# Gated-delta heads with beta as rows, two wide decay sums and block-wise inverse joins, and a relative-bias table written in eight pieces beside the weight loads

## The chip, the cores and the metric

The kernel runs on one core of a Trainium2 chip. The metric is the device time of one execution in microseconds (us), the median of several runs; lower is better. The core has five engines with a program each: TensorE (PE) multiplies matrices, VectorE (DVE), ScalarE (ACT) and GpSimd (POOL) work elementwise, and SyncE (SP) issues most of the transfers. Sixteen DMA engines carry the transfers between DRAM and the on-chip memory (SBUF); products land in PSUM.

## The reference, cut to what matters

An input x of 512 positions by 2048 features goes through three blocks in float32: (1) a gated recurrence and dilated attention, (2) spatial gating and neighbourhood attention, (3) a gated delta rule with 8 heads and sliding-window attention with 16 heads and a relative bias. Blocks 2 and 3 are modulated by `silu(c) @ w_ada + b_ada`. The change concerns parts of block 3:

```python
def gated_delta_rule_chunked(q, k, v, g, beta):
    g = jnp.cumsum(chunk(g), axis=-1)
    gdiff = g[..., :, None] - g[..., None, :]
    decay = jnp.where(causal, jnp.exp(jnp.where(causal, gdiff, 0.0)), 0.0)
    k_beta = k * beta[..., None]
    L = jnp.where(strict, einsum("bnhid,bnhjd->bnhij", k_beta, k) * decay, 0.0)
    t_inv = triangular_solve(eye + L, eye, lower=True, unit_diagonal=True)
    k_dec = k * jnp.exp(g_last[..., None] - g)[..., None]
    ...
def sliding_window_attention(q, k, v, sinks, rel_bias):
    bias = rel_bias[t5_bucket(jnp.maximum(dist, 0))]     # 32 buckets x 16 heads
    logits = where(valid, logits + bias, -inf)
    ...
```

## The kernel before, in words

All activations stand transposed, as 16 tiles of 128 features by 512 positions. Nearly all of PE's time goes into projections. `unit_steps` makes one tile of 128 outputs from 16 input tiles: two calls of `wchunk` each load 8 blocks of 128x128 weights (512 KB, `wr`, three buffers) on SP's queue; ACT rounds each half of 512 columns to `wh` (L114), DVE takes the rest as `wl` (L117; five halves of each fit), and PE multiplies three times per input tile (L128): `wh` by the high and the low part of the input, `wl` by the high one. A unit is 48 products of 128x512, a chunk 24.

`drive` runs a list of Python generators, one per head or gate. A generator yields either a unit that it needs or nothing; `drive` emits a unit's products, lets the waiting generators take a step between groups of 12 products, and so writes a head's small operations between the products of other units. The order of SP's queue, in which a transfer that waits holds up all behind it, comes out of the same program and the tile framework, which adds the waits for data and for buffers.

Beside this, each `wchunk` calls `bg()`, which takes one step of the first generator in `bgq`: before the change, `mods` for block 2 and then for block 3. Each of their steps loads 512 KB of `w_ada` (`gr`, two buffers) and adds it to `ga` (one buffer) on DVE.

`rel_bias` (L1279 on) is called at the start of `block2` (L798). It loads a one-hot table, the 32x16 bias and a mask, makes a 16x384 table of the biases by head and distance with one product and one sum, and writes each of the 16 rows 128 times to DRAM (`reld`, 16x128x384, 3 MB) with one DMA on ACT's queue. Much later `swa` (L1303 on) reads from `reld` with rows 383 apart, so that each of 128 positions finds its biases shifted by one.

In block 3, positions are in 4 chunks of 128 (`n`), and a tile of 128x512 holds the four chunks of a head side by side. `gdn_scalars` works out beta, g and the exponentials of its sums for all heads as columns (128 positions by 4 chunks x 8 heads). `gdn_k` (L1030 on) runs once per head: the keys are convolved, turned (`tr4`, four transposes, L134) and normalised to `kn`; POOL multiplies them by beta (`kb`) and by the decay to the chunk's end (`kd`); DVE multiplies a triangular matrix by g, chunk by chunk (`gt`); after two steps PE turns `kn` and `kb` and multiplies `later` (a constant triangle) by `gt` in four float32 products, whose exponential is the decay `dec`; then `at` is the strict triangle L. `inverse_blocks` solves the 32x32 diagonal blocks for two heads at a time on DVE, by way of DRAM (`du`, then `fs`; the result through `tm` to `dt`, and into `e0`). `inverse_join` joins these blocks to the inverse of 128x128: `c1` and `c2` are L with all but the blocks of one level set to zero, made on POOL by two mask products (L1128, L1129); each level is a chain of products of 128x128x128 in float32, four at a time, and sums on DVE. `gdn_scan` then goes through the four chunks of the head one after the other.

The functions that the change touches, and what calls them, with the line numbers of the profile:

Of the kernel before, what the change touches and what calls it, by code (L numbers as in the profile page):

```python
# [10 lines left out]
F32 = mybir.dt.float32  # L11
F32R = mybir.dt.float32r
# [3 lines left out]
OP = mybir.AluOpType  # L16
AX = mybir.AxisListType.X

P = 128
T = 512  # L20
# [20 lines left out]
class Kernel:  # L41
    def __init__(self, ctx, tc, A, outs, stop=99):
        self.tc, self.nc, self.A, self.O, self.stop = tc, tc.nc, A, outs, stop
        nc = self.nc
# [14 lines left out]
        C = self.A["const"]  # L59
# [17 lines left out]
        self.gld = self.dp.tile([2 * KT, P, T], F32, name="gld")  # L77
        self.reld = self.dp.tile([16, P, 384], F32, name="reld")
        self.res = self.dp.tile([KT, P, T], F32, name="res")


    def col(self, name, k=0, n=1):
# [475 lines left out]
                self.bg()  # L558

    def drain_bg(self):  # L560
        while self.bgq:
            self.bg()

    def mods(self, wada, c, b, mod):

# [229 lines left out]
    def block2(self, h, first):  # L795
        w = self.A["w2"]
        ys = [None] * 16
        self.rel_bias()  # L798
        todo = [self.sgu(g, h, w, ys) for g in range(8)]
        for p in range(8):  # L800
            todo.append(self.na(p, h, w, ys))
            if p:
                todo.append(self.gate(ys, 7 + p, w, 47 + p, h))
        todo.append(self.gate(ys, 15, w, 55, h))
        self.drive(todo, WIDTH2, done=first)
        return ys
# [157 lines left out]
    def gdn_scalars(self, ba):  # L964

        nc = self.nc
# [14 lines left out]
        self.log1p_cols(e, e)  # L981
        self.stt(gx, gx, 0.0, e, OP.max, OP.add)
        self.stt(c8(gx), c8(gx), -1.0, ea[:, None, :].to_broadcast([P, 4, 8]))
        ps = self.x()
        self.mm(ps[:, 0:32], self.triu, gx)
        self.mm(ps[:, 32:64], self.ones, gx)
        self.mm(ps[:, 64:96], self.later, gx)
        self.g, self.egc, self.egl, self.edl = gx, C("egc"), C("egl"), C("edl")
# [5 lines left out]
        self.ts(self.bh, beta, 0.5)  # L994

    def conv(self, ps, i):

# [31 lines left out]
    def gdn_k(self, hd, h, w, ks, free):  # L1029
        nc = self.nc  # L1030
        while not free():
            yield
        k = self.conv((yield w, 8 + hd, h), 8 + hd)
        yield
        yield
        kt = self.tr4(k)
        ss, rk = self.s(4), self.s(4)
        sq = self.t()
        self.act(sq, kt, AF.Square)
        nc.vector.tensor_reduce(ss, sq.rearrange("p (n t) -> p n t", t=P), AX, OP.add)  # L1040
# [24 lines left out]
        nc.gpsimd.affine_select(dec.rearrange("p (n t) -> p n t", t=P), dec.rearrange("p (n t) -> p n t", t=P),  # L1065
                                [[0, 4], [1, P]], OP.is_ge, 0.0, base=0, channel_multiplier=-1)
        yield
        gm = self.x()
        for n in range(4):
            c = slice(n * P, (n + 1) * P)  # L1070
            self.mm(gm[:, c], kf[:, c], kbf[:, c])
        at = self.y()
        self.tt(at, gm, dec)
        ks[hd] = kf, kd, dec, at

    def inverse_blocks(self, ats, e0s):
# [3 lines left out]
        nc = self.nc  # L1080
        self.n += 1
        B = 16 * len(ats)
        fs = self.gp.tile([P, 1024], F32, name=f"fs{self.n}", tag="gr", bufs=2)
        pr = self.gp.tile([P, 256], F32, name=f"fp{self.n}", tag="fp", bufs=1)
        tm = self.gp.tile([P, 256], F32, name=f"ft{self.n}", tag="ft", bufs=1)
        du = self.dp.tile([B, 1024], F32, name=f"du{self.n}")
# [30 lines left out]
                    e0s[a][32 * b:32 * b + 32, :].rearrange("c (n i) -> c n i", i=P)[:, :, 32 * b:32 * b + 32],  # L1117
                    dt[p0:p0 + 4].rearrange("n (c i) -> c n i", i=32))

    def inverse_join(self, at, e0):  # L1120

        nc = self.nc
        m = lambda i: self.mask_c[:, None, i * P:(i + 1) * P].to_broadcast([P, 4, P])
        v4 = lambda a: a.rearrange("p (n t) -> p n t", t=P)
        e, f = e0, self.t()
        nc.vector.transpose(f, e0)
        c1, c2 = self.t(), self.t()
        nc.gpsimd.tensor_tensor(v4(c1), v4(at), m(0), OP.mult)  # L1128
        nc.gpsimd.tensor_tensor(v4(c2), v4(at), m(1), OP.mult)  # L1129
        for lv, c in ((0, c1), (1, c2)):  # L1130
            yp, zp = self.x(), self.x()
            sl = [slice(n * P, (n + 1) * P) for n in range(4)]
            for q in sl:
                self.mm(yp[:, q], c[:, q], f[:, q])
            y = self.t()
            self.act(y, yp)
            yield
            for q in sl:
                self.mm(zp[:, q], y[:, q], e[:, q])
            if lv == 0:  # L1140
                zt = self.x()
                for q in sl:
                    self.mm(zt[:, q], e[:, q], y[:, q])
                f1, e1 = self.t(), self.t()
                self.tt(f1, f, zt, OP.subtract)
                self.tt(e1, e, zp, OP.subtract)
                f, e = f1, e1
                yield
            else:
                self.tt(e, e, zp, OP.subtract)  # L1150
        return e

    def gdn_qv(self, hd, h, w, ks, qs):
# [70 lines left out]
    def gdn(self, h, w, ys):  # L1224
# [18 lines left out]
        def scan(a):  # L1243
# [1 line left out]
                yield  # L1245
            kf, kd, dec, at = ks[a]
            q, rq, vb = qs[a]
            e = yield from self.inverse_join(at, f0s[a])
            yield
            ys[a] = yield from self.gdn_scan(a, kf, kd, e, q, rq, dec, vb)  # L1250

# [26 lines left out]

    def rel_bias(self):  # L1279
        nc = self.nc  # L1280
        ld, rb = self.t(), self.s(16)
        nc.sync.dma_start(ld[0:32, 0:384], self.A["rel1h"])
        nc.sync.dma_start(rb[0:32], self.A["rel"])
        mk = self.t()
        nc.sync.dma_start(mk[0:16, 0:384], self.A["relmask"])
        ps = self.x()
        self.mm(ps[0:16, 0:384], rb[0:32], ld[0:32, 0:384])
        self.tt(mk[0:16, 0:384], ps[0:16, 0:384], mk[0:16, 0:384], OP.add)
# [289 lines left out]
```

## Time and profile before

| | |
|---|---|
| runs, median (lowest to highest) | 3489.82 us (3487.78 to 3497.07), 3 runs |
| the profiled execution, its own time | 3486.6 us |
| its span in the profile | 3484.9 us |
| mean clock that PE was granted | 0.989 |
| moved by DMA | 449.39 MB |

The profile's first page gives each engine's busy time and share of the span, and the chain of work that ended last, as shares of the span by engine and line. Further views of the trace group instructions by line and tile, list the chain or the instructions in order of time, and give the busy times of a stretch. In them, a name such as `wl<-wr,wh` is the output and the inputs of an instruction by the program's tile names, L117 is a line of the kernel, `x4` is a count, and a float32 product appears as two records of PE. `PEld` is the load of weights into PE. In the rows of DMA issues the last number is the median time from issue to landing.

### The profile page before, as it was taken

The page shows a single profiled execution, that of the slowest core. Times are in us where ns is not written, and L with a number is a line of the kernel's source. Part 1 is how long each engine was busy: PE and PEld are TensorE (multiplying, and loading weights), DVE is VectorE, ACT ScalarE, POOL GpSimd, SP SyncE. Part 2 cuts the span into 40 slices and gives each one's busy share as a digit, 9 for nine tenths or more (in the row PEclk, how much of TensorE's full clock was granted, in tenths as well). Part 3 has the DMA queues.
Part 4 walks back from the last instruction along what each step waited for, and adds up shares of the span by engine and source line. Part 5 has one row for each costly group of instructions (what it writes and reads, how often), then busy time and mean ns, then how long its engine had stood idle before and what let it go on. Part 6 is the DMA issues. An engine that isn't in the chain of part 4 may idle for free.

```text
span 3484.9 us, 44515 instructions
## 1 busy us (share of the span) xinstructions
PE 3400.8 (98%) x16678; PEld 2841.0 (82%) x16678; DVE 2008.9 (58%) x3496; ACT 1273.6 (37%) x2439; POOL 322.9 (9%) x278
## 2 busy tenths in 40 slices
PE   8999999999999899999999999999999999999999
PEld 6878888888887788888888788787878888888887
DVE  8677656556767456644368767656754433344552
ACT  4222244444434222544442243232334443432331
POOL 3000000000341000101103201111110000000000
PEclk9999999999999999999999999999999999999999
DMA  6354355435564645522234233222222233324442
GB/s 219 115 169 158 129 167 177 142 131 184 199 218 134 154 161 187 172 87 91 87 102 145 91 120 91 88 90 79 81 70 79 91 102 101 128 97 145 144 142 91
DMA packets 157640, 449.39 MB, mean 129 GB/s; under 512 B 25792, under 2 KB 35824, under 8 KB 157424
## 3 DMA queue, kind: packets, MB, share of 16 engines
q1 hardware_dynamic: 155216, 442.96, 38.5%
q10 hardware_dynamic: 2208, 3.59, 0.8%
q8 instruction: 131, 2.15, 0.3%
q14 instruction: 85, 0.70, 0.1%
HBM read 421.31 MB, written 25.17 MB: 128 GB/s over the span
## 4 chain that ended last, share of the span: by engine, by line
PE 87%; DVE 6%; issue 3%; DMA 3%; POOL 1%; ACT 1%; SPq 0%; DVEq 0%; ACTq 0%; POOLq 0%
PE pm L128 75%; PE x L128 8%; DMA gr<-in_wada_dram 2%; PE x L134 2%; PE x L527 1%; DVE wl L117 1%; DVE t L117 1%; DVE ga L120 1%; DVE fp L117 1%; DMA wr<-in_w_dram 1%; DVE t L120 1%; DVE ft L1109 0%; POOL s L142 0%; DMA t<-in_xt_dram 0%; ACT t L114 0%
## 5 line engine op out<-in xcount | busy, mean ns | idle before, releaser
L128 PE MATMUL pm<-a,wh 128*128 128x512 f32 x8512 | 2673.4, 395 | 15.2 <-ACT a L114 15.2
L128 PEld LDWEIGHTS pm<-a,wh 128*128 128x128 f32 x8512 | 1578.4, 189 | 333.3 <-ACT a L114 17.2
L128 PE MATMUL pm<-a,wl 128*128 128x512 f32 x4256 | 1668.6, 392 | 8.7 <-DVE wl L117 8.7
L117 DVE TENSOR_TENSOR wl<-wr,wh 128x512 fp32r<-128x512 f32 (+1 forms) x1080 | 764.9, 711 | 1005.3 <-ACT wh L114 940.4
L114 ACT ACTIVATE wh<-wr 128x512 fp32r<-128x512 f32 (+1 forms) x1080 | 675.9, 628 | 1767.0 <-PE pm L128 1622.6
L128 PEld LDWEIGHTS pm<-a,wl 128*128 128x128 f32 x4256 | 803.0, 189 | 182.7 <-DVE wl L117 10.5
L120 DVE SCALAR_TENSOR_TENSOR ga<-gr,sc_c,ga 128x1024 f32<-128x1024 f32 x180 | 237.8, 1321 | 78.6 <-DMA gr<-in_wada_dram 78.2
L128 PEld LDWEIGHTS x<-t,t 128*128 128x128 f32 (+2 forms) x1488 | 187.9, 188 | 31.9 <-issue 9.4
L128 PE MATMUL x<-t,t 128*128 128x64 f32 (+3 forms) x1488 | 200.6, 277 | 5.2 <-DVE t L117 4.9
L114 ACT ACTIVATE t<-x 128x512 f32<-128x512 f32 (+3 forms) x325 | 155.8, 496 | 117.5 <-PE x L128 61.3
L142 POOL TENSOR_TENSOR s<-s,nhalf 128x4 f32<-128x4 f32 (+1 forms) x51 | 60.1, 1178 | 1289.8 <-DVE s L125 1258.3
L114 ACT ACTIVATE t<-t 128x512 f32<-128x512 f32 (+1 forms) x172 | 106.8, 630 | 134.2 <-DVE t L120 83.2
L117 DVE TENSOR_TENSOR t<-t,t 128x512 f32<-128x512 f32 (+1 forms) x195 | 137.8, 707 | 23.0 <-ACT t L114 19.0
L114 ACT ACTIVATE t<-t,s 128x128 f32<-128x128 f32 (+2 forms) x192 | 98.6, 514 | 79.4 <-DVE s L438 60.2
L134 PE MATMUL x<-cst,t 128*128 128x128 f32 x496 | 74.3, 276 | 24.0 <-ACT t L114 9.8
L134 PEld LDWEIGHTS x<-cst,t 128*128 128x128 f32 x496 | 60.6, 142 | 40.0 <-ACT t L114 10.2
L597 POOL TENSOR_TENSOR acc<-acc,t 128x512 f32<-128x512 f32 x42 | 75.7, 1828 | 85.4 <-DVE t L120 71.3
L117 DVE TENSOR_TENSOR a<-t,a 128x512 fp32r<-128x512 f32 x112 | 79.3, 727 | 4.6 <-ACT a L114 4.4
L527 PE MATMUL x<-cst,t 128*128 128x128 f32 x464 | 74.5, 275 | 4.6 <-ACT t L114 4.6
L748 POOL TENSOR_TENSOR t<-cst,t 128x256 f32<-128x256 f32 x48 | 41.2, 891 | 351.7 <-DMA t<-in_rpb_dram 274.2
L114 ACT ACTIVATE t<-pm 128x512 f32<-128x512 f32 (+2 forms) x154 | 68.6, 482 | 13.5 <-PE pm L128 13.3
L120 DVE SCALAR_TENSOR_TENSOR t<-t,pm 128x512 f32<-128x512 f32 x64 | 43.7, 684 | 46.4 <-PE pm L128 46.0
(216 smaller groups left out, 1815.6 us busy)
## 6 DMA issues: line engine op xcount, KB each, us to landing
wr<-in_w_dram SPq DMA_DIRECT2D x380, 512.0 KB, 3.3
gr<-in_wada_dram SPq DMA_DIRECT2D x192, 512.0 KB, 4.2
wr<-in_wo_dram SPq DMA_DIRECT2D x96, 512.0 KB, 3.4
wr<-in_w_dram SPq DMA_DIRECT2D x48, 256.0 KB, 2.9
t<-in_xt_dram SPq DMA_DIRECT2D x32, 256.0 KB, 4.0
res<-t SPq DMA_DIRECT2D x32, 256.0 KB, 2.2
t<-res SPq DMA_DIRECT2D x32, 256.0 KB, 2.8
gld<-t SPq DMA_DIRECT2D x32, 256.0 KB, 2.0
```

Source lines behind the costliest of these rows:

```text
L114: return self.nc.scalar.activation(out, in_, fn, **kw)
L117: return self.nc.vector.tensor_tensor(out, a, b, op)
L120: return self.nc.vector.scalar_tensor_tensor(out, a, s, b, op0=op0, op1=op1)
L128: return self.nc.tensor.matmul(out, l, r, start=start, stop=stop, skip_group_check=True)
L134: self.nc.tensor.transpose(b[:, p * P:(p + 1) * P], src[:, p * P:(p + 1) * P], self.ident)
L142: self.nc.gpsimd.tensor_tensor(out, u, self.nhalf[:, :n], OP.pow)
L527: self.nc.tensor.transpose(b[:, j * P:(j + 1) * P], pr[:, j * P:(j + 1) * P], self.ident)
L597: self.nc.gpsimd.tensor_tensor(self.acc[i], self.acc[i], src, OP.add)
L748: nc.gpsimd.tensor_tensor(rows(nbs[hh][cb]), self.mask_na[:, None, v * 32:v * 32 + 32].to_broadcast([P, 8, 32]), sv[:, :, off:off + 32], O ...
```

## The change

The diff, cut to its core:

```diff
     def drain_bg(self):
-        while self.bgq:
-            self.bg()
+        for q in self.bgq:
+            for _ in q:
+                pass
+        self.bgq = []
...
     def block2(self, h, first):
-        self.rel_bias()
...
     def gdn_scalars(self, ba):
+        pads = self.gp.tile([P, 1024], F32, name="pads", tag="gr", bufs=2)
+        nc.gpsimd.memset(pads, 0.0)
+        self.pads = [pads[:, 0:T], pads[:, T:]]
+        gr = self.gp.tile([P, 1024], F32R, name="later_r", tag="gr", bufs=2)
+        self.later_r, self.ghl = gr[:, 0:P], [gr[:, P:P + 32], gr[:, P + 32:P + 64]]
+        nc.vector.tensor_copy(self.later_r, self.later)
+        nc.vector.tensor_copy(self.ghl[0], gx)
+        self.tt(self.ghl[1], gx, self.ghl[0].bitcast(F32), OP.subtract)
...
+        nc.tensor.transpose(pt[0:32, 0:P], beta, self.ident)
+        nc.vector.tensor_copy(rt[0:32, 0:P], pt[0:32, 0:P])
+        nc.sync.dma_start(self.betad.rearrange("n h t -> (n h) t"), rt[0:32, 0:P])
+
+    def beta_row(self, hd):
+        r = self.t()
+        src = self.betad
+        self.nc.sync.dma_start(r.rearrange("p (n t) -> p n t", t=P),
+                               bass.AP(tensor=src.tensor, offset=src.offset + hd * P,
+                                       ap=[[0, P], [8 * P, 4], [1, P]]))
+        return r
...
     def gdn_k(self, hd, h, w, ks, free):
+        br = self.beta_row(hd)
...
-        kb = self.t()
-        nc.gpsimd.tensor_tensor(kb.rearrange("p (n d) -> p n d", d=P), kn.rearrange("p (n d) -> p n d", d=P),
-                                self.hc(self.beta, hd)[:, :, None].to_broadcast([P, 4, P]), OP.mult)
-        kd = self.y()
-        nc.gpsimd.tensor_tensor(kd.rearrange("p (n d) -> p n d", d=P), kn.rearrange("p (n d) -> p n d", d=P),
-                                self.hc(self.edl, hd)[:, :, None].to_broadcast([P, 4, P]), OP.mult)
-        gt = self.t()
-        for n in range(4):
-            self.ts(gt[:, n * P:(n + 1) * P], self.triu, self.g[:, 8 * n + hd:8 * n + hd + 1])
+        gts = [self.t("w", F32R) for _ in range(2)]
+        for gt, g in zip(gts, self.ghl):
+            self.tt(gt.rearrange("p (n t) -> p n t", t=P), self.triu[:, None, :].to_broadcast([P, 4, P]),
+                    self.hc(g, hd).bitcast(F32)[:, :, None].to_broadcast([P, 4, P]))
         yield
         yield
         kf, kbf = self.y(), self.t()
         self.act(kf, self.tr4(kn))
-        self.act(kbf, self.tr4(kb))
...
-        for n in range(4):
-            c = slice(n * P, (n + 1) * P)
-            self.mm(gb[:, c], self.later, gt[:, c])
+        for i in range(2):
+            self.mm(gb, self.later_r, gts[i], start=i == 0, stop=i == 1)
...
+        self.tt(kbf, kf, br)
+        kd = self.y()
+        self.rows(kd, kn, self.hc(self.edl, hd))
...
     def inverse_blocks(self, ats, e0s):
-        fs = self.gp.tile([P, 1024], F32, name=f"fs{self.n}", tag="gr", bufs=2)
+        fs = self.gp.tile([P, 1024], F32, name=f"fs{self.n}", tag="ga", bufs=1)
...
-    def inverse_join(self, at, e0):
-        nc.gpsimd.tensor_tensor(v4(c1), v4(at), m(0), OP.mult)
-        nc.gpsimd.tensor_tensor(v4(c2), v4(at), m(1), OP.mult)
-        for lv, c in ((0, c1), (1, c2)):
...
+    def inverse_join(self, at, e, c):
+        f = self.t()
+        nc.vector.transpose(f, e)
+        for r in (0, 64):
+            self.act(v4(c)[r:r + 32, :, r + 32:r + 64], v4(at)[r:r + 32, :, r + 32:r + 64])
+        yp, zp, zt = self.x(), self.x(), self.x()
+        for q in sl:
+            self.mm(yp[:, q], c[:, q], f[:, q])
+        self.act(y, yp)
+        yield
+        for n, q in enumerate(sl):
+            self.mm(zt[:, n * P:n * P + 64], e[:, q], y[:, n * P:n * P + 64])
+        for q in sl:
+            self.mm(zp[:, q], y[:, q], e[:, q])
+        self.ts(v4(f)[32:64, :, 0:32], v4(zt)[32:64, :, 0:32], -1.0)
+        for r in (0, 64):
+            self.ts(v4(e)[r:r + 32, :, r + 32:r + 64], v4(zp)[r:r + 32, :, r + 32:r + 64], -1.0)
+        yield
+        for n in range(4):
+            self.mm(b[64:128, 64 * n:64 * n + 64], at[0:64, n * P + 64:n * P + P], f[0:64, n * P:n * P + 64])
+        self.act(y2[64:128, 0:256], b[64:128, 0:256])
+        yield
+        for n in range(4):
+            self.mm(b[0:64, 64 * n:64 * n + 64], y2[64:128, 64 * n:64 * n + 64], e[64:128, n * P + 64:n * P + P])
+        self.ts(v4(e)[0:64, :, 64:128], b[0:64, 0:256].rearrange("p (n t) -> p n t", t=64), -1.0)
...
     def rel_bias(self):
+        buf = self.gp.tile([P, 1024], F32, name="relb", tag="ga", bufs=1)
+        mk, ld, rb = buf[0:16, 0:384], buf[0:32, 384:768], buf[0:32, 768:784]
...
+        yield
+        yield
...
-        nc.scalar.dma_start(self.reld, mk[0:16, None, 0:384].to_broadcast([16, P, 384]))
+        for i in range(0, 16, 2):
+            yield
+            nc.sync.dma_start(self.reld[i:i + 2], buf[i:i + 2, None, 0:384].to_broadcast([2, P, 384]))
...
     def run(self):
+        self.bgq.append(self.rel_bias())
         h, first = self.out1(self.block1())
         h, first = self.out2(self.block2(h, first))
+        self.drain_bg()
```

In words. Beta goes to DRAM once (`betad`, 16 KB), and each head reads its row into all 128 partitions, so that it can be multiplied into the turned keys; four transposes and a copy per head fall away, and both products with beta and with the end decay move from POOL to DVE. g is split into a high and a low fp32r part, and the four float32 products of the decay sum become two fp32r products of 512 columns. The first level of the join takes its blocks by two ACT copies into tiles that were set to zero once; the second level multiplies 64x64 blocks only, and results are written, negated, just where they belong. The buffer `fs` of the solves moves to the tag `ga`, of which there is one. `rel_bias` becomes the third background generator: it starts when both `mods` are done, in block 2's attention part, and issues its eight pieces of two rows each (384 KB) on SP's queue, one per background step.

What SP issues there now, in the order of its program (`wr_...` are weight loads, with the program's number; the three `relb` loads are the table's inputs, and `t<-in_rpb_dram` belongs to the neighbourhood attention). First up to the load 12756:

```order
L157 DMA wr_12664<-in_w_dram 128x1024
L157 DMA wr_12701<-in_w_dram 128x1024
L1307 DMA relb<-in_rel1h_dram 32x384
L1308 DMA relb<-in_rel_dram 32x16
L1309 DMA relb<-in_relmask_dram 16x384
L746 DMA t_12744<-in_rpb_dram 128x384
L157 DMA wr_12756<-in_w_dram 128x1024
L746 DMA t_12750<-in_rpb_dram 128x384
```

And right behind these rows:

```order
L157 DMA wr_12838<-in_w_dram 128x1024
L157 DMA wr_12924<-in_w_dram 128x1024
L1318 DMA reld<-relb 256x1x384 x4
L157 DMA wr_12974<-in_w_dram 128x1024
L1318 DMA reld<-relb 256x1x384
L157 DMA wr_13035<-in_w_dram 128x1024
L1318 DMA reld<-relb 256x1x384
L157 DMA wr_13070<-in_w_dram 128x1024
L1318 DMA reld<-relb 256x1x384
L157 DMA wr_13118<-in_w_dram 128x1024
L1318 DMA reld<-relb 256x1x384
L157 DMA wr_13153<-in_w_dram 128x1024
```

Before, the same place of SP's queue holds weight loads alone (`wr_12757` there is `wr_12756` above), and the one write stands in ACT's queue at the start of block 2, between two of its copies. First SP, then ACT:

```order
L156 DMA wr_12757<-in_w_dram 128x1024
L156 DMA wr_12838<-in_w_dram 128x1024
L156 DMA wr_12923<-in_w_dram 128x1024
L156 DMA wr_12972<-in_w_dram 128x1024
L156 DMA wr_13032<-in_w_dram 128x1024
L156 DMA wr_13066<-in_w_dram 128x1024
```
```order
L114 ACTIVATE t_9301<-pm_8825 128x512
L114 ACTIVATE t_9376<-pm_8826 128x512
L1290 DMA reld<-t_9259 2048x1x384
L114 ACTIVATE t_9417<-pm_9327 128x512
L114 ACTIVATE wh_512_9430<-wr_9424 128x512
```

Four pieces stand together behind the load 12924, and each of the four loads after it, 12974 to 13118, has one more piece behind it; the load 13153 has all eight ahead of it. PE multiplies the bias table between the weights of two chunks; `wh_0_12666` below is the first half of the load 12664:

```order
L129 MATMUL pm_12578<-a_9194,wh_512_12623 128x512
L129 MATMUL pm_12578<-a_9193,wl_512_12624 128x512
L129 MATMUL x_12674<-relb 16x384
L129 MATMUL pm_12663<-a_8833,wh_0_12666 128x512
L129 MATMUL pm_12663<-a_8834,wh_0_12666 128x512
```

So the sum that the first piece waits for can be made when PE begins the chunk of 12664, and the loads 12664, 12701, 12756, 12838 and 12924 stand ahead of the pieces in SP's queue.

The second place is PE at the key step of the first head. Before (`t_17378` is `kn`, `t_17380` is `kb`, `t_17384` is `gt`):

```order
L128 MATMUL pm_17330<-a_16688,wl_512_17396 128x512
L134 MATMUL x_17425<-cst,t_17378 128x128 x4
L134 MATMUL x_17431<-cst,t_17380 128x128 x4
L128 MATMUL x_17437<-t_17384,cst 128x128 x4
L128 MATMUL pm_17453<-a_16313,wh_0_17456 128x512
```

And now:

```order
L129 MATMUL pm_17347<-a_16694,wl_512_17410 128x512
L135 MATMUL x_17439<-cst,t_17397 128x128 x4
L129 MATMUL x_17445<-t_17399,later_r 128x512
L129 MATMUL x_17445<-t_17400,later_r 128x512
L129 MATMUL pm_17462<-a_16319,wh_0_17465 128x512
```

Twelve small PE instructions between the units' products became four small and two wide ones.

More of the change, by code (lines that the diff above doesn't have):

```diff
@@ L79, in __init__ @@
         self.res = self.dp.tile([KT, P, T], F32, name="res")
+        self.betad = self.dp.tile([4, 8, P], F32, name="betad")
     def col(self, name, k=0, n=1):
@@ L987, in gdn_scalars @@
         self.mm(ps[:, 64:96], self.later, gx)
-        self.g, self.egc, self.egl, self.edl = gx, C("egc"), C("egl"), C("edl")
+        self.egc, self.egl, self.edl = C("egc"), C("egl"), C("edl")
         self.act(self.egc, ps[:, 0:32], AF.Exp)
@@ L994, in gdn_scalars @@
         self.ts(self.bh, beta, 0.5)
+        pt, rt = self.x(), self.t()
+        nc.tensor.transpose(pt[0:32, 0:P], beta, self.ident)
[8 more added lines that the diff above has]
+        return r
     def conv(self, ps, i):
@@ L1118, in inverse_blocks @@
                     dt[p0:p0 + 4].rearrange("n (c i) -> c n i", i=32))
-    def inverse_join(self, at, e0):
+    def inverse_join(self, at, e, c):
         nc = self.nc
-        m = lambda i: self.mask_c[:, None, i * P:(i + 1) * P].to_broadcast([P, 4, P])
         v4 = lambda a: a.rearrange("p (n t) -> p n t", t=P)
[L1125 to L1128, printed above, removed]
-        nc.gpsimd.tensor_tensor(v4(c2), v4(at), m(1), OP.mult)
-        for lv, c in ((0, c1), (1, c2)):
[L1131 to L1150, printed above, removed]
@@ new lines, in inverse_join @@
+        f = self.t()
[3 more added lines that the diff above has]
+        yp, zp, zt = self.x(), self.x(), self.x()
+        sl = [slice(n * P, (n + 1) * P) for n in range(4)]
+        for q in sl:
+            self.mm(yp[:, q], c[:, q], f[:, q])
+        y = self.t()
+        self.act(y, yp)
+        yield
+        for n, q in enumerate(sl):
+            self.mm(zt[:, n * P:n * P + 64], e[:, q], y[:, n * P:n * P + 64])
@@ new lines, in inverse_join @@
+        for q in sl:
[4 more added lines that the diff above has]
+        yield
+        b = self.x()
+        y2 = self.t()
+        for n in range(4):
+            self.mm(b[64:128, 64 * n:64 * n + 64], at[0:64, n * P + 64:n * P + P], f[0:64, n * P:n * P + 64])
+        self.act(y2[64:128, 0:256], b[64:128, 0:256])
@@ L1151, in inverse_join @@
+        yield
+        b = self.x()
+        for n in range(4):
+            self.mm(b[0:64, 64 * n:64 * n + 64], y2[64:128, 64 * n:64 * n + 64], e[64:128, n * P + 64:n * P + P])
+        self.ts(v4(e)[0:64, :, 64:128], b[0:64, 0:256].rearrange("p (n t) -> p n t", t=64), -1.0)
         return e
@@ L1247, in scan @@
             q, rq, vb = qs[a]
-            e = yield from self.inverse_join(at, f0s[a])
+            e = yield from self.inverse_join(at, f0s[a], self.pads[a % 2])
             yield
@@ L1280, in rel_bias @@
         nc = self.nc
[L1281 to L1285, printed above, removed]
-        ps = self.x()
-        self.mm(ps[0:16, 0:384], rb[0:32], ld[0:32, 0:384])
-        self.tt(mk[0:16, 0:384], ps[0:16, 0:384], mk[0:16, 0:384], OP.add)
-        nc.scalar.dma_start(self.reld, mk[0:16, None, 0:384].to_broadcast([16, P, 384]))
+        buf = self.gp.tile([P, 1024], F32, name="relb", tag="ga", bufs=1)
+        mk, ld, rb = buf[0:16, 0:384], buf[0:32, 384:768], buf[0:32, 768:784]
+        nc.sync.dma_start(ld, self.A["rel1h"])
+        nc.sync.dma_start(rb, self.A["rel"])
+        nc.sync.dma_start(mk, self.A["relmask"])
+        yield
+        yield
+        ps = self.x()
+        self.mm(ps[0:16, 0:384], rb, ld)
+        self.tt(mk, ps[0:16, 0:384], mk, OP.add)
+        for i in range(0, 16, 2):
+            yield
+            nc.sync.dma_start(self.reld[i:i + 2], buf[i:i + 2, None, 0:384].to_broadcast([2, P, 384]))
     def swa_k(self, i, h, w, kf, scale):
```

## The prediction

> **What bounds the kernel now.** I read the page's busy shares first, then the chain of work that ended last, then the places where the chain leaves TensorE (PE).
>
> ```profile
> PE 3400.8 (98%) x16678; PEld 2841.0 (82%) x16678; DVE 2008.9 (58%) x3496; ACT 1273.6 (37%) x2439; POOL 322.9 (9%) x278
> PE 87%; DVE 6%; issue 3%; DMA 3%; POOL 1%; ACT 1%; SPq 0%; DVEq 0%; ACTq 0%; POOLq 0%
> ```
>
> PE is the bound: 3484.9 - 3400.8 = 84 us of idle in the whole span. So an edit pays in two ways only: it shortens work in PE's queue, or it shortens one of the few waits. The profiled execution took 3486.6 us, of which 1.7 lie outside the span; the median of the runs is 3489.8, 0.1% above it. All sums are made against 3486.6.
>
> Two waits matter here. The first stands at the start of block 2, in the chain in order of time and in the busy times by stretch (columns: PE, PEld, DVE, ACT, POOL busy, granted clock, share of the DMA engines, GB/s):
>
> ```profile
> 1145.38 1.92 DVE wl L117 x4
> 1147.30 18.08 DMA wr<-in_w_dram
> ...
> 1148.00:1156.00 8.00, 8.00 (x38) 6.60 (x36) 0.47 (x1) 0.00 (x0) 0.00 (x0) 1.00 0.88 101
> 1156.00:1167.00 11.00, 1.19 (x6) 0.73 (x5) 1.99 (x3) 2.67 (x5) 0.00 (x0) 0.68 0.82 221
> 1167.00:1172.00 5.00, 5.00 (x18) 4.09 (x17) 3.43 (x14) 0.59 (x2) 1.01 (x1) 0.68 0.47 166
> ```
>
> A weight load took 16 to 18 us, because the DMA engines were 88% busy with something else at only 101 GB/s. PE lived on converted weights until 1156 and then sat idle for 11.00 - 1.19 = 9.8 us; afterwards its clock was 0.68 for 5 us, that is half speed for some 3.2 us, another 1.6 us lost. The something else is the relative-bias write on the ACT queue (q10), beside what the same load takes in a free moment:
>
> ```profile
> q10 hardware_dynamic: 1006, 1.55, 87.6%
> reld<-t ACTq DMA_DIRECT2D x1, 3072.0 KB
> wr<-in_w_dram SPq DMA_DIRECT2D x5, 512.0 KB, 9.9
> wr<-in_w_dram SPq DMA_DIRECT2D x380, 512.0 KB, 3.3
> ```
>
> The first row is the queue in the 15 us from 1130 to 1145: 1006 rows of 1536 bytes kept 87.6% of 16 engines, so one row held its engine for 0.876 * 16 * 15 / 1006 = 209 ns; the whole of it, 3072 KB at 101 GB/s, is 31 us.
>
> The second place is the gated-delta stage:
>
> ```profile
> 2100.00:2624.00 524.00, 501.52 (x2643) 423.69 (x2642) 351.21 (x730) 168.93 (x303) 74.28 (x83) 0.99 0.26 82
> PE x L134 <- DVE t L120: 6.4, 1, 6.4
> 2183.18 0.18 DVE L117 TENSOR_TENSOR fp<-ft,fs 128x16 f32<-128x16 f32 x1 [4.14 <-POOL ft L1099]
> 2183.69 1.63 POOL L1128 TENSOR_TENSOR t<-t,cst 128x512 f32<-128x512 f32 x1
> 2184.09 1.28 DVE L117 TENSOR_TENSOR fp<-ft,fs 128x24 f32<-128x24 f32 x1
> 2185.62 1.02 DVE L117 TENSOR_TENSOR fp<-ft,fs 128x32 f32<-128x32 f32 x1
> ```
>
> PE idles 22.5 of 524 us there. The longest wait, 6.4 us, is for VectorE (DVE), whose small products take 1.28 and 1.02 us while GpSimd (POOL) multiplies the masks, after 0.18 us just before.
>
> **The change, part by part.**
>
> *Relative bias taken out of the start of block 2.* The ACT-queue write goes, and the wait of 9.8 us and the slow clock of 1.6 us with it: -11.4 us. The load that was late is issued at 1146.1 and, at 3.3 us, lands six microseconds before PE runs dry. Bounds: 0, if another wait takes its place, and -13.
>
> *Decay sums and key products, per head.* In PE's timeline a head's key step reads:
>
> ```profile
> 2108.75 1.03 PE L134 MATMUL x<-cst,t 128*128 128x128 f32 x8
> 2109.62 1.06 PE L128 MATMUL x<-t,cst 128*128 128x128 f32 x8
> 2110.43 0.48 PE L128 MATMUL pm<-a,wh 128*128 128x512 f32 x1
> 1532.43 24.52 PE pm L128 x108
> ```
>
> From start to start, eight transposes take 0.87 us, and the four decay sums 0.81 (each float32 product is two records). Four transposes go: 0.43. Two wide products at 24.52 / 108 = 0.227 us take the place of 0.81: 0.36 saved. Eight heads times 0.79: -6.3 us, all in PE's queue. On DVE two wide products replace four narrow ones and two products come over from POOL; their cover is DVE's 33% of idle time in this stage. The row of betas is a 256 KB load per head on SP, issued two steps ahead of its use:
>
> ```profile
> t<-gld SPq DMA_DIRECT2D x32, 256.0 KB, 2.9
> ```
>
> Another load of that size lands in 2.9 us, and a step is twelve products of 0.227 us, so the two steps hide it and I cost it at nothing. If that cover fails it holds up DVE for a microsecond or two per head.
>
> *Inverse joins.* There are 20 products before and 20 after. What shrinks is their width, and a narrower one is not cheaper:
>
> ```profile
> 1417.99 1.00 PE L128 MATMUL x<-t,t 128*128 128x64 f32 x8
> 1418.82 0.61 PE L527 MATMUL x<-cst,t 128*128 128x128 f32 x4
> ```
>
> Eight records of 64 columns take 0.83 us, as against 0.81 to 0.87 for 128. Products with 64 rows and 64 weight columns in a burst are not in the trace: free at best, which saves 16 records * 0.104 * 8 heads = 13 us, and 0 at worst. I take -1, by the nearest row.
>
> *Waits of this stage.* The mask products leave POOL, so the 6.4 us wait loses its two stretched DVE steps, some 2 us. Against that, the loads of the second solve now wait for the first solve to end, since they share one buffer. I take -4, between +8 (a few waits like that one again) and -15.
>
> *The relative-bias rows, in eight pieces.* They move to block 2's attention part, onto SP's queue, which also carries every weight load. The order in the part on the change shows four pieces together, then one ahead of each of the next four loads. What does one piece cost? It has 256 rows of 1536 bytes, but its outer dimension is 2, where the old write had 16. The trace has one other DMA with a small outer dimension, the store of the solved blocks (L1112, outer dimension 4). The queue's row for half a microsecond in which that store was alone:
>
> ```profile
> 2178.47 0.66 SPq L1112 DMA_DIRECT2D dt<-ft  x1
> DMA packets 16, 0.02 MB, mean 33 GB/s; under 512 B 0, under 2 KB 16, under 8 KB 16
> q1 hardware_dynamic: 16, 0.02, 22.9%
> ```
>
> 22.9% of 16 engines is 3.7: four of them worked, twelve stood still, while the write with 16 kept 88% busy. So I take it that a piece runs on two engines, 128 rows on each. The time of a row lies between the crowded 209 ns above and an unhindered one, from a quiet stretch of weight loads:
>
> ```profile
> 2300.00:2320.00 20.00, 20.00 (x90) 16.57 (x89) 7.51 (x12) 6.12 (x10) 0.00 (x0) 1.00 0.28 92
> ```
>
> 0.28 of 16 engines for 92 GB/s is 49 ps per byte, so 75 ns for 1536 bytes and 199 for 4096. Sixteen readers crowded the old write and two crowd a piece, so I choose a value nearer to the free one: 110 ns. A piece is then 128 * 110 = 14.1 us, eight are 113 us one after the other if they share the same two engines, which I take, and every weight load behind them in the queue needs those two as well.
>
> [...]
>
> What hides it? PE computes the bias just ahead of load 12664's weights. From there PE has five chunks whose loads were issued before the pieces (12664 to 12924), and the four that follow (12974 to 13118) are loaded between pieces. The period of a chunk comes from the next like point of the chain:
>
> ```profile
> 1584.71 24.52 PE pm L128 x108
> ```
>
> From 1532.43 (quoted above) it is 52.28 us for four units of two chunks, 6.53 us each. Nine chunks are 58.8 us of cover. The load behind the last piece (13153) is usable after 113 + 5 loads * 8 rows * 0.2 us (8) + 1.5 (product, sum, issue) + 1.7 (landing) + 0.6 (conversion) = 124.8 us. PE is short by 66 us, in some five waits, and loses about 1.6 more to the clock at the end, as at 1167. Cost: +67 us. Bounds: 75 ns per row give 77 + 12 - 59 + 2 = +32; 209 ns give 214 + 12 - 59 + 2 = +169; all sixteen engines, at the old write's 31 us in all, give 0.
>
> **Sum.** 3486.6 - 11.4 - 6.3 - 1 - 4 + 67 = **3531 us**, slower by 1.2% of the median.
>
> **The rivals.**
>
> *The pieces hide (faster).* If a piece ran on all 16 engines, or each on a pair of its own, eight would take some 31 us, less than the cover. The point from which it decides is (58.8 - 11.8) / 8 = 5.9 us per piece: below, PE never waits. Then only the gains stay: 3486.6 - 22.7 = 3464.
>
> ```profile
> gr<-in_wada_dram SPq DMA_DIRECT2D x192, 512.0 KB, 4.2
> ```
>
> For it speaks that 192 such loads, each larger than a piece, ran through the same queue and landed in 4.2 us; against it the 22.9%.
>
> *Crowded rows.* A row costs 209 ns whoever else reads: 3486.6 - 22.7 + 169 = 3633. Against it: the old crowd was sixteen engines.
>
> *Free rows.* 75 ns: 3486.6 - 22.7 + 32 = 3496, no change that can be seen. [...]
>
> *DVE becomes the bound of the gated-delta stage.* It takes two products from POOL, and in the worst stretches it is 96% busy (19.14 of 20 us):
>
> ```profile
> 2360.00:2380.00 20.00, 18.44 (x87) 14.37 (x85) 19.14 (x45) 4.29 (x8) 0.00 (x0) 1.00 0.30 93
> ```
>  With the pieces hidden and two waits like the 6.4 us one more, 3464 + 4 + 13 = 3481.
>
> *The joins do not get shorter on PE.* That is my forecast already (-1 of a possible -13).
>
> **How the numbers follow.** The forecast, two engines at 90 to 140 ns a row, 3510 to 3562 by the same sum: 0.64. Free rows, 3485 to 3510: 0.13. Crowded rows, above 3562: 0.07. The pieces hide, 3452 to 3479: 0.12. Hidden, but DVE binds, about 3481: 0.04. The measurement can tell about 0.3%, 10 us, from no change. Faster by more than that, below 3479: 0.12. Within it, up to some 3500: the DVE case and two thirds of the free rows, 0.13. Slower: 0.75. The range runs from 3470 to 3570: the forecast, the free rows, the DVE case and the nearer edges of the other two, about 0.84. The forecast's own range is 3510 to 3562.
>
> **What would show it.** Right: after the relative-bias product, PE idle for tens of microseconds with the wait put down to `wr<-in_w_dram`, DMA engines about an eighth busy (2 of 16) in that stretch, the load behind the four pieces landing after 50 us or more; no late load at the start of block 2; two wide products of 0.45 us per head. Wrong: pieces landing within 6 us, or loads that land while pieces are still under way. The forecast fails most easily on the time of a row on two engines, then on the cover of nine chunks.

## The result, and the profile after

| | before | after |
|---|---|---|
| median of the runs, us | 3488.8 (4 runs, 3482.8 to 3497.07) | 3524.02 (4 runs, 3518.53 to 3526.41) |
| ratio to before, 95% interval | | 1.0101 [1.0087, 1.0115] |
| profiled execution, us | 3486.6 | 3518.53 |

The changed kernel is 1.0% slower. The first page of its profile gives the busy time of each engine and the shares of the chain that ended last:

```profile
PE 3394.8 (97%) x16599; PEld 2828.4 (80%) x16599; DVE 1997.4 (57%) x3508; ACT 1274.8 (36%) x2447; POOL 285.9 (8%) x247
PE 86%; DVE 6%; DMA 4%; issue 1%; SPq 1%; ACT 1%; POOL 0%; DVEq 0%; ACTq 0%; POOLq 0%
```

PE has 6 us less to do than before and is idle for 3516.8 - 3394.8 = 122 us, where it was 84. The projections are the same 12960 products in both kernels, in the same order, so the two traces can be laid beside each other: the start of a given product after, less its start before, shows where time is won or lost (worked out from the starts of the products in the traces, us):

| part of the program | change there |
|---|---|
| up to the old write (no edit acts there) | -7.8 |
| start of block 2, the old write | -13.2 |
| block 2 up to the bias product | +1.4 |
| the eight pieces | +73.9 |
| from there to the gated-delta stage | -0.2 |
| gated-delta stage | -21.8 |
| to the end | -0.1 |
| sum | +32.3 |

The first line is the scatter of single executions: in the profiles of the experiments below, that point came from 1.4 us earlier to 9.5 us later than in the profile of before, with the same instructions ahead of it. So the parts below are compared between like products, and whole kernels by the ratio of their runs.

The chain of work in order of time (start, length, what) at the place of the pieces; L1318 is their line:

```profile
1523.80 0.55 DVE relb L118
...
1524.37 0.79 SPq L1318
1525.16 0.06 issue
1525.21 4.73 SPq L1318
1529.94 0.04 issue
1529.99 15.20 SPq L1318
1545.19 0.04 issue
1545.23 15.01 SPq L1318
...
1560.35 91.12 DMA wr<-in_w_dram x5
...
1652.23 1.22 PE pm L129 x2
```

The third and the fourth piece hold SP for 15.2 and 15.0 us. By the pace of the rows below a piece takes 15.4 us, so I read the length of these issues as the time of a piece; that the queue takes no more until earlier rows are gone is my guess at the reason and was not tried by itself. The later pieces are issued in about 2 us each, but there the weight load ahead of each one holds SP, for 13 to 15 us. Then the chain is five weight loads, 91 us, until PE goes on at 1652.2. What PE does meanwhile, by its rows in order of time (in brackets the idle time before and what ended it), and then the waits and the busy times of that stretch (columns of the last row: stretch, length, PE, PEld, DVE, ACT, POOL, granted clock, share of the DMA engines, GB/s):

```profile
1589.45 1.22 PE L129 MATMUL pm<-a,wh 128*128 128x512 f32 x2 [28.97 <-ACT wh L115]
...
1593.22 0.62 PE L129 MATMUL pm<-a,wh 128*128 128x512 f32 x2
...
1605.67 1.22 PE L129 MATMUL pm<-a,wh 128*128 128x512 f32 x2 [8.86 <-ACT wh L115]
...
1621.11 1.22 PE L129 MATMUL pm<-a,wh 128*128 128x512 f32 x2 [7.69 <-ACT wh L115]
```
```profile
ACT wh L115 <- DMA wr<-in_w_dram: 65.4, 6, 27.5
...
PE pm L129 <- ACT wh L115: 60.3, 5, 29.0
```
```profile
1550.00:1660.00 110.00, 48.91 (x179) 37.86 (x179) 18.77 (x28) 15.92 (x35) 6.43 (x6) 0.67 0.24 70
```

Five waits, 60.3 of 110 us, put down to ACT's conversion, which itself waited 65.4 us for the loads. And the DMA queue of SP in 10 us (1530 to 1540) in which nothing but pieces moved: packets, MB, share of 16 engines:

```profile
q1 hardware_dynamic: 166, 0.25, 11.3%
```

11.3% of 16 is 1.8 engines; 166 rows in 10 us on two of them are 120 ns a row, and 256 rows at that pace are 15.4 us.

At the start of block 2 nothing is late any more. The old stretch in the changed kernel, and the loads in it:

```profile
1140.00:1170.00 30.00, 30.00 (x138) 24.82 (x137) 12.28 (x29) 7.81 (x14) 1.01 (x1) 0.95 0.29 94
wr<-in_w_dram SPq DMA_DIRECT2D x5, 512.0 KB, 3.2
```

The clock column of this profile reads 0.95 here, where PE is never idle; in the profile before it reads 1.00 in such a place. The products do not show a difference: 320 us of the same work (from 1180 before, from 1159 after) keep PE busy for 319.5 and 319.1 us. So I take nothing from that column when I compare these two profiles.

The key step and a join of the gated-delta stage, from the chain in order of time:

```profile
2162.93 0.45 PE x L135 x4
2163.38 0.46 PE x L129 x2
...
2245.91 1.11 PE x L129 x8
2247.03 0.93 PE pm L129 x4
2247.96 2.43 PE x L129 x24
2250.38 1.38 PE pm L129 x5
2251.76 0.60 PE x L129 x8
```

Four transposes and two wide products now take 0.91 us, where eight transposes and four float32 sums took 1.68. The second level of a join, eight records of 64x64, takes 0.60, where eight of 128x128 took 0.81 to 0.87.

### The profile page after: what moved, and what is told of

Read it like the earlier page. It is cut to its first block, busy times and chain, and to the rows that moved or that the text cites. A ratio compares the mean times of both kernels' runs of the same rounds, so it can differ in the third digit from the quotient of the medians.

```text
span 3516.8 us, 44344 instructions
## 1 busy us (share of the span) xinstructions
PE 3394.8 (97%) x16599; PEld 2828.4 (80%) x16599; DVE 1997.4 (57%) x3508; ACT 1274.8 (36%) x2447; POOL 285.9 (8%) x247
## 4 chain that ended last, share of the span: by engine, by line
PE 86%; DVE 6%; DMA 4%; issue 1%; SPq 1%; ACT 1%; POOL 0%; DVEq 0%; ACTq 0%; POOLq 0%
PE pm L129 75%; PE x L129 8%; DMA wr<-in_w_dram 3%; PE x L135 2%; DMA gr<-in_wada_dram 1%; PE x L528 1%; DVE wl L118 1%; SPq L1318 1%; DVE t L118 1%; DVE fp L118 1%; DVE t L121 1%; DVE ft L1130 1%; DVE ga L121 1%; ACT t L115 0%; ACT wh L115 0%
## 5 line engine op out<-in xcount | busy, mean ns | idle before, releaser
L129 PE MATMUL pm<-a,wh 128*128 128x512 f32 x8512 | 2677.2, 396 | 75.4 <-ACT wh L115 60.3
L129 PEld LDWEIGHTS x<-t,t 128*128 128x128 f32 (+3 forms) x1296 | 156.2, 183 | 26.6 <-issue 6.5
L129 PE MATMUL x<-t,t 128*128 128x64 f32 (+5 forms) x1296 | 167.7, 274 | 3.6 <-DVE t L118 3.6
L115 ACT ACTIVATE t<-t 128x512 f32<-128x512 f32 (+1 forms) x172 | 106.8, 630 | 120.5 <-DVE t L121 73.9
L129 PE MATMUL x<-acc,t 128*128 128x128 f32 (+3 forms) x336 | 72.8, 310 | 0.0
```

Source lines behind the costliest of these rows:

```text
L115: return self.nc.scalar.activation(out, in_, fn, **kw)
L129: return self.nc.tensor.matmul(out, l, r, start=start, stop=stop, skip_group_check=True)
```

## The experiments

Each ratio is to runs of the kernel before on the same chip. The theory at the start: the pieces cost what they do because few DMA engines serve them, with every weight load queued behind; the rest of the change gains. That the few engines set the pace did not hold, as the rows apart show.

**The relative-bias edit alone.** The kernel before, with only this:

```diff
-        self.rel_bias()                      # in block2
+        self.bgq.append(self.rel_bias())     # in run, rel_bias as in the change
```

> The kernel before with the relative-bias edit alone (third background generator, eight pieces on SP's queue); the gated-delta stage is as before. Theory: the pieces cost what the trace of the changed kernel shows between like products (73.9 us from the bias product on, less 13.2 us at the start of block 2), whatever the gated-delta stage does: 3488.8 + 61 = 3550 us, PE idle for some 60 us in several waits behind the pieces. Rival: the stall comes out of the whole change (buffers shared by the new parts): then near 3477 us.

Measured: 3553.57 us, 1.0176 [1.0151, 1.0200]. Between like products the pieces cost 72.9 us and the start of block 2 gained 13.2. The cost does not come out of the gated-delta edits.

**The gated-delta edits alone.** The changed kernel with the old `rel_bias`:

```diff
-        self.bgq.append(self.rel_bias())
+        self.rel_bias()                      # in block2, one write on ACT's queue
```

> The changed kernel with rel_bias put back as it was (one write on ACT's queue at the start of block 2); the gated-delta edits stay. Theory: the gated-delta stage keeps its 22 us of gain and the old wait at the start of block 2 comes back: 3488.8 - 22 = 3467 us. Rival: part of those 22 us is the luck of one execution (an unchanged part before block 2 was 7.8 us shorter as well): 3474 to 3478 us, which would be the forecast's own 11.3 us.

Measured: 3467.96 us, 0.9932 [0.9911, 0.9952]. The gain is 22 us rather than the forecast 11.3: 538.0 us for the stage in its profile, and 538.7 in that of the changed kernel, against 560.4 before.

**One write in place of eight.**

```diff
-        for i in range(0, 16, 2):
-            yield
-            nc.sync.dma_start(self.reld[i:i + 2], buf[i:i + 2, None, 0:384].to_broadcast([2, P, 384]))
+        yield
+        nc.sync.dma_start(self.reld, buf[0:16, None, 0:384].to_broadcast([16, P, 384]))
```

> The changed kernel with one DMA of all 16 rows (outer dimension 16) at the place of the first piece, same queue, same bytes. Theory (the outer dimension of 2 leaves two engines at work): 16 engines, near 31 us for the whole, hidden by the five loads ahead of it but for a few us: 3524 - 70 = 3454 us, between 3448 and 3462; DMA engines 80 to 90% busy in that stretch. Rival (what costs is that 3 MB stand ahead of the loads in SP's queue): 3515 to 3524 us.

Measured: 3451.49 us, 0.9891 [0.9866, 0.9915]. The same bytes in the same queue at the same place cost 2.8 us. The queue's row for 1532 to 1542:

```profile
q1 hardware_dynamic: 650, 1.00, 88.0%
```

650 rows in 10 us, against 166. So it is the shape, not the place in the queue.

**Rows eight apart.** Eight pieces again, but each of two rows whose partitions in SBUF are eight apart:

```diff
-        for i in range(0, 16, 2):
-            nc.sync.dma_start(self.reld[i:i + 2], buf[i:i + 2, None, 0:384]...)
+        for i in range(8):
+            nc.sync.dma_start(self.reld[i:i + 9:8], buf[i:i + 9:8, None, 0:384]...)
```

> The changed kernel with pieces of rows i and i+8 in place of i and i+1: as many pieces, bytes and rows, an outer dimension of 2 as before, but the two source partitions are eight apart. Theory A (the row's time of about 119 ns is set by the two engines or by the broadcast row itself): 15.2 us per piece and 3524 us as before. Theory B (two neighbouring partitions share one door of SBUF, which held the piece at 393 KB in 15.2 us, 26 GB/s): rows near the free 75 ns, pieces of 9.6 us, stall 32 us in place of 74: 3482 us, between 3475 and 3492.

Measured: 3466.26 us, 0.9928 [0.9907, 0.9949], and the pieces cost 17.9 us between like products. 1535 to 1545 in its queue:

```profile
q1 hardware_dynamic: 328, 0.50, 13.3%
```

The pieces came faster than theory B had them, 7.8 us (256 rows at 328 in 10 us) in place of 9.6, and the time lies below its range. Still two engines, and twice the rows: 61 ns each, less than the "free" 75 ns that I had taken from the weight loads. So the number of engines was not what set the pace of a piece. One thing was not yet separate: here the destination is in two parts, in the changed kernel in one.

**Rows two apart, rows four apart.** As above, with i and i+2 (0 and 2, 1 and 3, 4 and 6, ...), and with i and i+4 (0 and 4, 1 and 5, ...):

```diff
+        for i in (0, 1, 4, 5, 8, 9, 12, 13): ... self.reld[i:i + 3:2], buf[i:i + 3:2, ...]
+        for i in (0, 1, 2, 3, 8, 9, 10, 11): ... self.reld[i:i + 5:4], buf[i:i + 5:4, ...]
```

> The changed kernel with pieces of rows i and i+2 (0 and 2, 1 and 3, 4 and 6, ...). With rows eight apart a piece took 7.7 us in place of 15.2, but its destination was then also in two parts and not in one. Theory A (rows of the same four neighbouring partitions share one way out of SBUF): 15 us per piece again, 3515 to 3528 us. Theory B (the destination in one part is what was slow): 7.7 us per piece, 3462 to 3472 us.

> The changed kernel with pieces of rows i and i+4 (0 and 4, 1 and 5, 2 and 6, ...). Theory A (groups of four partitions): 7.7 us per piece, 3462 to 3472 us. If the groups were of eight: 15 us per piece, 3515 to 3528 us.

Measured: 3536.30 us, 1.0128 [1.0108, 1.0148], and 3474.86 us, 0.9953 [0.9937, 0.9969]; the first is 8 us above the range of theory A and the second 3, and between like products the pieces cost 79.3 and 17.8, the latter as with rows eight apart. The queue in 10 us of pieces, first two apart (1547 to 1557), then four apart (1548 to 1558):

```profile
q1 hardware_dynamic: 160, 0.24, 11.2%
```
```profile
q1 hardware_dynamic: 331, 0.50, 13.3%
```

The destination is in two parts in both. Rows 0 and 2 halve the pace, rows 0 and 4 do not: partitions 0 to 3 share something, and 4 is outside.

**Four rows at a time.** Twice the engines, and still one group of four partitions:

```diff
-        for i in range(0, 16, 2): ... self.reld[i:i + 2], buf[i:i + 2, ...].to_broadcast([2, P, 384])
+        for i in range(0, 16, 4): ... self.reld[i:i + 4], buf[i:i + 4, ...].to_broadcast([4, P, 384])
```

> The changed kernel with four pieces of four neighbouring rows in place of eight of two (outer dimension 4, so twice the engines; all four stand ahead of the load that had four pieces ahead of it). Theory A (the way out of the four partitions at 25 GB/s sets the pace, not the number of engines): 31 us per piece, 124 us for all, 22% of the DMA engines busy; the load behind them waits for all of it, 124 us less some 33 us of cover: 3451 + 90 = 3541 us. Theory B (the number of engines sets it): four engines, 50 GB/s, 62 us for all, 3451 + 28 = 3479 us.

Measured: 3542.62 us, 1.0144 [1.0127, 1.0161]; 89.2 us between like products. 1544 to 1554:

```profile
q1 hardware_dynamic: 162, 0.25, 21.7%
```

21.7% of 16 is 3.5 engines, and they move the same 0.25 MB in 10 us. A group of four partitions gave 25 GB/s to two engines and to four; the write of 16 rows reads four such groups, 1.00 MB in 10 us.

**The pieces on ACT's queue.** No weight load stands behind them there:

```diff
-            nc.sync.dma_start(self.reld[i:i + 2], ...)
+            nc.scalar.dma_start(self.reld[i:i + 2], ...)
```

> The changed kernel with the eight pieces issued on ACT's queue, so that no weight load stands behind them. Theory A (only some two pieces fit into a queue, then the issue itself holds its engine for the 15 us of a piece, as SP was held from the third piece on; ACT also makes every high half of the weights): PE waits for ACT instead, 3500 to 3530 us. Theory B (the loads go ahead beside the pieces, two engines being only a little slower): 3450 to 3456 us. Theory C (ACT is not held, but the loads share the two busy engines and land late): 3465 to 3495 us.

Measured: 3501.48 us, 1.0046 [1.0032, 1.0060]. ACT's rows in order of time (its queue is ACTq):

```profile
1558.57 10.96 ACTq L1318 DMA_DIRECT2D reld<-relb  x1
1558.91 0.58 ACT L115 ACTIVATE t<-x 128x512 f32<-128x512 f32 x1
1569.63 0.51 ACT L115 ACTIVATE t<-t,s 128x256 f32<-128x256 f32 x1 [10.14 <-issue]
```

From the third piece on the issue holds ACT for 8.5 to 14.9 us, and ACT makes the weights' high halves. The loads beside the pieces landed in 8.8 us (the median) in place of 3.3, but ACT waited only 6.2 us for them, so theory A holds. The pieces cost 49.7 us here between like products: the wait has another place, and is only a third smaller.

**Fewer copies.** `swa` needs row p shifted by p. With p = 8a + b, rows 376 apart for a and 383 apart for b give the same shifts out of 23 copies of a row:

```diff
-        self.reld = self.dp.tile([16, P, 384], F32, name="reld")
+        self.reld = self.dp.tile([16, 23, 384], F32, name="reld")
...
-                  offset=src.offset + hd * P * 384 + 127, ap=[[383, P], [1, 256]]
+                  offset=src.offset + hd * 23 * 384 + 127, ap=[[376, 16], [383, 8], [1, 256]]
```

and one write of 16 rows at the place of the first piece.

> The changed kernel with 23 copies of each bias row in DRAM in place of 128 (0.57 MB), written by one DMA of 16 rows at the place of the first piece; swa reads position p = 8a + b at a*376 + b*383, the same values. Expected: the write takes 6 us in place of 31, nothing waits for it: 3448 to 3454 us, faster than before by about 1.1% and no slower than the one write of 3 MB.

Measured: 3449.96 us, 0.9898 [0.9883, 0.9912]. It beats both kernels, and is not to be told from the one write of 128 copies, of which all but 2.8 us was hidden already; here nothing of the write is left between like products.

This write also answers a rival that the pieces leave open. In all of them a row that is near in SBUF is near in DRAM as well, so the place that they write to could have set their pace. Here 16 rows go into 0.57 MB of DRAM, less than the 0.79 MB that one piece of four rows fills. The queue from 1540 to 1545:

```profile
q1 hardware_dynamic: 327, 0.50, 87.4%
```

327 rows in 5 us are 100 GB/s, as with 3 MB. So nearness in DRAM does not make a piece slow; of the two, the partitions that it reads are what is left.

**The parts of the gated-delta edits.** First the key step (beta rows, decay sums, key products) with the old joins, then the new joins with the old key step; the solves' buffer `fs` has its single copy in both (the two lines with # stand for the other edits):

```diff
+        fs = self.gp.tile([P, 1024], F32, name=f"fs{self.n}", tag="ga", bufs=1)
+        # key step of the change, inverse_join of before (first kernel)
+        # inverse_join of the change, gdn_k of before (second kernel)
```

> The kernel before with the decay sums, the beta rows and the key products of the change, but with the old joins (mask products on POOL, 128x128 products) and the old relative-bias write; the solves' buffer is the one that the change gives them. The two gated-delta parts together gave 20.4 us between like products in one profile, 10.4 of it around the first solve. Theory A (that wait goes with the mask products, so with the joins): 6 to 9 us less than before, 3481 to 3484. Theory B (it goes with the key step's work, or with the buffer): 16 to 18 us less, 3472 to 3475.

> The kernel before with the new joins alone (and the solves' buffer of the change); key step, decay sums and relative-bias write as before. Theory A: 12 to 15 us less than before, 3475 to 3478, with the 6.4 us wait at the first join gone. Theory B: 3 to 5 us less, 3485 to 3488, with that wait still there.

Measured: 3477.82 us, 0.9972 [0.9963, 0.9982], and 3473.72 us, 0.9963 [0.9951, 0.9976]. The second lost 14.3 us, as its theory A had it. The first lost 10.2, between its two theories. But the 6.4 us wait was gone in both, so it does not go with the joins as such. What the two kernels share is the buffer, so the last kernel is the one before with that line alone:

```diff
-        fs = self.gp.tile([P, 1024], F32, name=f"fs{self.n}", tag="gr", bufs=2)
+        fs = self.gp.tile([P, 1024], F32, name=f"fs{self.n}", tag="ga", bufs=1)
```

> The kernel before with one edit: the solves' buffer fs has one copy (tag ga), as in the change, so that the second solve's loads wait for the end of the first; all else as before. With either gated-delta part alone the stage lost 8 to 10 us around the first solve, and this edit was in both. Theory A (the shared buffer itself takes the second solve out of VectorE's way while the next convolution waits, and the 6.4 us wait goes with it): that wait is below 3 us, the stage 5 to 10 us shorter, 3479 to 3484 us. Theory B (the forecast's: the later loads can only cost): the wait stays or grows, 3488 to 3496 us.

Measured: 3481.12 us, 0.9983 [0.9974, 0.9992], theory A. VectorE in order of time, first before, then with one buffer (`fp<-ft,fs` are steps of the second solve, `t<-pm,par,t` those of a convolution that PE waits for):

```profile
2183.18 0.18 DVE L117 TENSOR_TENSOR fp<-ft,fs 128x16 f32<-128x16 f32 x1 [4.14 <-POOL ft L1099]
...
2188.44 0.27 DVE L117 TENSOR_TENSOR fp<-ft,fs 128x64 f32<-128x64 f32 x1
...
2189.36 0.73 DVE L120 SCALAR_TENSOR_TENSOR t<-pm,par,t 128x511 f32<-128x511 f32 x1
```
```profile
2191.02 1.53 DVE L120 SCALAR_TENSOR_TENSOR t<-pm,par,t 128x511 f32<-128x511 f32 x2
2192.53 0.09 DVE L1101 MEMSET fs<- 128x32 f32 x1
...
2193.85 0.17 DVE L117 TENSOR_TENSOR fp<-ft,fs 128x16 f32<-128x16 f32 x1
```

With two buffers the second solve's steps stand ahead of the convolution; with one, the convolution comes first. The stage in five profiles, between the same products each time (columns as above; before, one buffer, key step, joins, and all the gated-delta edits with the old `rel_bias`):

```profile
2062.90:2623.30 560.40, 537.18 (x2802) 452.96 (x2801) 367.91 (x784) 179.28 (x326) 74.28 (x83) 0.99 0.27 84
```
```profile
2071.30:2625.30 554.00, 535.46 (x2802) 451.42 (x2801) 368.02 (x785) 179.51 (x327) 74.13 (x83) 0.99 0.27 85
```
```profile
2066.70:2614.90 548.20, 527.74 (x2724) 441.74 (x2722) 368.21 (x788) 175.50 (x319) 60.31 (x67) 1.00 0.29 90
```
```profile
2068.20:2613.50 545.30, 534.39 (x2802) 447.06 (x2801) 352.00 (x792) 182.88 (x341) 52.44 (x67) 0.99 0.27 86
```
```profile
2065.00:2603.00 538.00, 524.71 (x2723) 436.36 (x2721) 353.52 (x796) 179.37 (x334) 37.99 (x51) 1.00 0.30 92
```

The buffer gives 560.4 - 554.0 = 6.4 us. On top of it the key step gives 5.8: PE is busy for 7.7 us less (535.5 to 527.7), and idle for 1.9 more. The joins give 8.7, of which PE's idle time makes 7.6 (18.5 to 10.9). The three add up to 20.9 of the 22.4. By PE's time the 22.4 are 12.5 us less of busy time (537.2 to 524.7) and 9.9 less of idle time (23.2 to 13.3).

## Why the prediction was right, point by point

- **Sign and size: right.** 3531 was forecast, 3524 measured. Two terms were off and nearly cancelled: the pieces cost 7 us more than forecast, and the gated-delta stage gained some 10 more. That the sum came this close is in part luck.
- **The eight pieces (+67): right in mechanism, 7 us short, with the wrong owner of the pace.** Two engines (11.3% of 16 is 1.8), five waits (60.3 us), the loads behind the pieces: all there. That all eight pieces use the same two engines was assumed, and no run shows which engines served a piece; what the trace shows is 1.8 of them busy from 1530 to 1540, when the second piece had been issued and the first, at 15.4 us, was not yet done. The term that was mis-sized is the 110 ns of a row: 120 were measured, 15.2 us for a piece in place of 14.1, which is 9 us for the eight. The load behind the last piece was to be usable 124.8 us after the bias product; PE went on with it at 1652.2, 129.5 us after 1522.7, so some 4 us of the other terms were not needed. I set the row's price between free and crowded engines. The experiments say that the engines were not the bound: two rows of one group of four partitions move at 25 GB/s together, and two engines do 61 ns on rows of two groups. No term of the sum asked which partitions a piece reads.
- **The clock after waits (+1.6): seen after each of the five waits**, not after the last alone: two records take 1.22 us at first, 0.62 later. The loads set the time there, so I take it that all but the last of these slow stretches only took the place of idle time; that was not tried by itself. The 73.9 are 60.3 us of idle time in the five waits, 12.2 by which the projections of that stretch were slower (91.3 us from start to start, idle time left out, in place of 79.1), and small items.
- **Pieces that hide (3464): refuted for these pieces, true for the one write.** At 31 us (2048 rows at 650 in 10 us) all but 2.8 us of it hid, as the point of decision said it would. With each row of a piece in a group of its own, 7.8 us a piece, part of the wait stayed (17.9 and 17.8 us between like products), since the point was 5.9.
- **The start of block 2 (-11.4): right**, -13.2.
- **Decay sums and key products (-6.3): right.** 0.77 us per head on PE in place of 0.79. PE's small products in the stage take 102.8 us with one buffer and 96.4 with the key step (from start to start, idle time left out), 6.4 less.
- **Joins (-1): the second level is cheaper than I took it.** 0.60 us for eight records against 0.83 for the nearest row; two such groups a head make some 3.7 us by the rows. PE's small products, taken as above, show 3.5 (102.8 to 99.3). Its busy time shows only 1.1 (535.5 to 534.4), since the one profile with the joins holds 32 projections slower than 0.5 us and the one it is compared with 10.
- **Waits of the stage (-4): the term that failed.** PE's idle time in the stage fell by 9.9 us: the single buffer took 4.7 (the rest of its 6.4 is busy time; the stage holds 10 projections slower than 0.5 us in place of 18), the joins 7.6, and the key step gave 1.9 back. The step that was wrong is the sentence that the second solve's loads wait for the first "against" the gain. A later start put the solve behind a convolution that PE needs, and that was the gain. The mask products did cost, as the row of 1.28 us said, but in other places: at 2544.4 in the profile before, a DVE product beside one of them took 1.75 us where the next took 0.68, PE waited 2.1 us for it, and with the new joins that wait is gone.
- **DVE as the bound: refuted.** With the key step, and so with two products a head more on DVE, the stage became shorter, 548.2 us in place of 554.0. The key step by itself did add 1.9 us of idle time on PE.

## What to carry to other kernels

Before a transfer is cut into pieces, look at which partitions of SBUF and how many DMA engines each piece reaches: a piece that reads one group of four neighbouring partitions moved at 25 GB/s here, and what was queued behind it waited for it: the loads on SP's queue, for which PE stood idle for 60.3 us in all, or the issuing engine itself, ACT, for up to 14.9 us a piece. Cut across the groups (17.8 us lost here in place of 73.9), or don't cut: one write of the same bytes was hidden but for 2.8 us. And read a change in a buffer's count as a change in order: one buffer fewer made this kernel faster, 6.4 us in its stage, since the work that it held back had been in the way of a product that PE waited for.

## What the runs showed of the hardware that had not been expected

- The pace of a broadcast out of SBUF went with the group of four partitions and not with the engines: 166 rows of 1536 bytes in 10 us for two rows of one group on two engines, 162 for four rows on four engines, 328 and 331 for two rows of two groups on two engines, 650 for 16 rows on 16. Into a fifth of the DRAM, 16 rows kept the same pace, 327 in 5 us.
- The issue of a DMA can hold its engine for as long as a piece takes: 15.2 us on SP, for the third piece, and up to 14.9 on ACT, from the third on (256 rows each, 15.4 us by the pace of 166 rows in 10 us).
- A DVE step of 128x24 beside a POOL product of 128x512 took 1.28 us, where the step of 128x16 before it took 0.18; with one buffer it took 1.06.
